# Modulation units inside an RWKV-7 stage: four k-tiles per transfer, their four products as one group

## The chip, the cores and the metric

The kernel runs on one core of a Trainium2 chip. The metric is the device time of one execution in microseconds (us); the median of three executions before the change is 2456.73 us. Below, PE is the matrix engine (TensorE), PEld its weight loads, DVE VectorE, ACT ScalarE, POOL GpSimd, and SP the engine whose queue issues most transfers (DMAs) from DRAM.

## The reference

One layer of a hybrid model on 256 latent tokens and 256 context tokens of width 2048. A vector `c` scales, shifts and gates the layer's branches (modulation):

```
mod_lat = jnp.split((silu_c @ w_mod[i] + b_mod[i])[:, None, :], 6, axis=-1)
u_lat = _modulate(_rmsnorm(x, g_norm1[i]), mod_lat[0], mod_lat[1])
...
x = x + mod_lat[2] * y_lat
v_lat = _modulate(_rmsnorm(x, g_norm2[i]), mod_lat[3], mod_lat[4])
x = x + mod_lat[5] * _moe(v_lat, *moe_p)
```

`w_mod` is a float32 matrix of 2048 x 12288, 96 MB. Its first third (`mod_lat[0]`, `mod_lat[1]`) is needed before anything else. The other two thirds, 64 MB, are needed only after the token mixer, and that part is what the change touches. The token mixer has three branches: S5 (a state-space scan), RWKV-7 (a recurrence with a 64 x 64 state for each of 16 heads, in two directions) and gated linear attention; a mixture of experts follows.

## The kernel before

The program is written as Python generators that yield after each small piece of work. `merge` runs several of them side by side: it always steps the one that has done the smallest share of the steps it is taken to have. The order so written is only a preference. A scheduler behind it puts the instructions of each engine into a fixed order, taking what it believes to be ready first, in the order of writing among those. Each engine then works through its own list strictly in order and waits at semaphores.

**The RWKV-7 stage** (`rwkv`) merges five streams, over 18 steps and one before them:

- `dense`: products of the normed tokens with columns of `w_in`. `split` loads a block of four k-tiles of weights (`ww`, 256 KB, line 346, on SP), ACT casts it to a shortened float `hw` (line 348), DVE forms the remainder `lw` (line 353), and PE multiplies three times for each k-tile (lines 384 to 386). The pools hold four raw blocks, three `hw` and three `lw`, so loads and splits run some blocks ahead of PE, and a load waits until an earlier block has been split.
- `rw_build1` and `rw_build2`: the operators of a half (one channel tile, latents or context), small products on PE with much work on DVE, ACT and POOL between them.
- `rw_chain`: the recurrence of the half before, a chain that goes through PE, DVE and POOL for every chunk of 32 tokens.
- `mods`: the rest of the modulation.

**`mods`** handles 16 units, each 512 columns of `w_mod`. The vector silu(c) is the stationary operand, as one column in a window of 32 columns (`self.sil[:, k, win]`); the weights stream past it. The array is used in four column groups of 32: k-tile k goes to the group `k % 4`, written `tile_position=(0, 32 * j)`, and its result is added in the quadrant `pt[32 * j:32 * j + 32]` of one PSUM bank. Unit u lands in row u of each quadrant, because the window is shifted by u. For each unit, eight blocks of two k-tiles (`wm`, 512 KB each, line 952) come in on SP. Two places rotate for them (`wm=2` in `BUFS`). In every other block of the first 15 units, the two k-tiles are scaled and added first, on ACT (line 956) and DVE (line 957), and one product with a column of ones (`self.one`, line 960) follows:

```
nc.scalar.activation(w[:, 1], w[:, 1], AF.Copy, scale=c[1])
nc.vector.scalar_tensor_tensor(w[:, 1], w[:, 0], c[0], w[:, 1], op0=OP.mult, op1=OP.add)
```

The other blocks have two products, one for each k-tile (line 969). Each product is float32 and shows as two records in the trace. So there are 60 blocks with one product and 68 with two: 196 products in 128 places of PE's list. `rwkv` gives `mods` 18 of its steps in each step of the stage (`chainv(mods, 18)`), and a unit has 17.

The first third of the modulation is done by `mod_unit` at the start of the program, with the same products (line 254) and no sums.

Of the kernel before, what the change touches and what calls it, by code (L numbers as in the profile page):

```python
# [11 lines left out]
AF = mybir.ActivationFunctionType  # L12
OP = mybir.AluOpType
# [7 lines left out]
# columns of the packed per-channel parameters  # L21
# [15 lines left out]
def mergeg(*streams):  # L37
    """Runs generators side by side, each given with the number of steps it is taken to have."""
    live = [[g, 0, max(n, 1)] for g, n in streams if g is not None]
    while live:  # L40
        s = min(live, key=lambda x: x[1] / x[2])
        try:
            next(s[0])
            s[1] += 1
            yield
        except StopIteration:
            live.remove(s)
# [7 lines left out]
# places of the blocks of the experts' weights: first pool, later pool, and those that lend their place at the start  # L55
MW, MWB, MWC = 14, 3, 3
# tiles that rotate
BUFS = dict(raw=4, wh=3, wl=3, wm=2, dl=3, z=2, kb=2, vz=2, t1=2, S=2, lmk=2, lmr=2, dup=2, ar0=2)
# [11 lines left out]
def chainv(g, n):  # L70
    """the first n steps of a generator"""
    for _ in range(n if g is not None else 0):
        if next(g, StopIteration) is StopIteration:
            return
        yield


def late(g, n):
    """a generator after n empty steps"""
    if g is None:  # L80
        return
    for _ in range(n):
        yield
    yield from g


class Pool:
    """tiles that share a place by name"""
# [8 lines left out]
# where a tile lives, if not among RWKV-7's  # L97
TOP = ("pp", "ident", "ones", "eps", "id32", "hsel")
MID = ("hka", "hb", "nmu", "omk", "sil", "one")
# [6 lines left out]
class Kern:  # L106
# [29 lines left out]
    # ---------------------------------------------------------------- constants  # L136
    def consts(self):
# [14 lines left out]
        # ident folded on 32 columns: 1 where the column is the partition modulo 32  # L152
# [3 lines left out]
        # rows of the two heads of a channel tile  # L156
# [8 lines left out]
        # the latents' in a column of zeros, for windows that put it into a row of its own  # L165
# [3 lines left out]
        self.one = self.t([128, 47], "one")  # L169
        nc.vector.memset(self.one, 0.0)  # L170
        nc.vector.memset(self.one[:, 15:16], 1.0)
        # derived parameters
# [10 lines left out]
    def rwkv_consts(self):  # L183
        nc = self.nc
        # sum of the free index and the partition: 127 on the other diagonal
# [3 lines left out]
        # position within a chunk: partition modulo 32 (pr) and column modulo 32 (cr)  # L189
# [8 lines left out]
        # parity of the quadrant: 1 even, -1 odd  # L198
# [6 lines left out]
        # source on the partition, target on the column: strictly before (0, 1); not after (2, 3), minus where the  # L205
        # removed keys lie
# [6 lines left out]
        # the diagonal, for each parity  # L213
# [4 lines left out]
        # blocks of 16: the same; below the diagonal, row block odd, column block the one before it  # L218
# [13 lines left out]
        # the diagonal of blocks  # L232
# [4 lines left out]
        # restarts of the running sum, every 32 tokens  # L237
# [4 lines left out]
    # ---------------------------------------------------------------- modulation  # L242
    def mod_unit(self, pt, n):
        """pt[32j + r, :] = silu(c_r) . w_mod[:, 512 n ...] over the k-tiles of group j"""
# [13 lines left out]
    def mod_out(self, pt, n):  # L258
        """the unit's columns on partitions, into modT"""
# [10 lines left out]
    def phase_a(self, jobs):  # L270
# [12 lines left out]
        def norm():  # L283
            # root mean squares of the tokens, on every partition
# [19 lines left out]
        # the first columns of w_in as far as the normed tokens are there  # L304
# [36 lines left out]
    # ---------------------------------------------------------------- dense products  # L341
    def split(self, src, shape, name):
        """A block of weights from DRAM as two float32r parts whose sum it is."""
# [6 lines left out]
        # now and then on Pool, where the vector engine has more to do  # L350
# [5 lines left out]
    def dense(self, jobs, nk=16, xs=None, kb=4):  # L356
        """Columns of products as channels on partitions. Jobs: (source [128, nk, m] by k-tiles, n, evac(psum)) with n
        tokens; the blocks of weights are split ahead of their products."""
# [32 lines left out]
    # ---------------------------------------------------------------- RWKV-7  # L391
    def mix(self, z, ns, col, tag):
        """z + (prev - z) mu for both directions, the second with its time reversed.
        z [128, ns, 258] has a zero before and after each sequence; the result [128, ns, 2, 256]."""
# [15 lines left out]
    def rw_lo(self):  # L410
        """the low-rank inputs of decay and learning rate"""
        def ev(pt):
# [5 lines left out]
            # in two parts one below the other, per head of the two  # L418
# [11 lines left out]
    def wcol(self, name, i, n, evac, m=128):  # L430
        """a job of dense: columns of w_in, [2, 128, 8, m]"""
# [3 lines left out]
    def rw_cols(self, ct):  # L435
        """key, value and receptance of a channel tile"""
# [7 lines left out]
    def rank_up(self, ct):  # L444
        """the second factors of decay and learning rate for a channel tile, in two parts"""
# [9 lines left out]
    def rw_build1(self, ct, s):  # L455
        """chunk operators of the two heads of a channel tile: s = 0 the latents, 1 the context.
        Chunk c of a row of four (j): what belongs to the keys lies in quadrant c, what belongs to the removed keys
        in quadrant c ^ 1, so that both are neighbours in the half that holds c, in the tile e = c % 2."""
# [10 lines left out]
        # gates of this channel tile  # L469
# [9 lines left out]
        # sigmoid(x) = (1 + tanh(x / 2)) / 2; the second is kept as its tanh  # L479
# [6 lines left out]
        # the key that is removed, and the inverse square of its norm  # L486
# [14 lines left out]
        # running log decay of each chunk, and its exponentials  # L501
# [13 lines left out]
        # alpha, and rho beside it for the latents, the chunks in the order 1 0 3 2 ...  # L515
# [8 lines left out]
        # the key scaled by the learning rate  # L524
# [3 lines left out]
        # beta: the removed key over its squared norm, times the learning rate  # L528
# [21 lines left out]
        # products of the keys with alpha (0, 1) and rho (2 + e), sources on partitions, masked by time  # L550
# [22 lines left out]
        if lat:  # L573
            # the bonus of the current token joins the diagonal
# [7 lines left out]
        # kappa and minus beta in the frame of the chunk's end: [e][j][half][slot][t]  # L582
# [12 lines left out]
    def rw_build2(self, ct, s):  # L595
        """the rest of them: rows by token, the inverse of the removed keys' products and what goes through it"""
# [25 lines left out]
        # the four chunks of a row side by side, zero elsewhere  # L622
# [9 lines left out]
        # removed values of the chunk's own: (alpha kappa) v, alpha beside it  # L632
# [7 lines left out]
        # inverse of 1 + L, transposed: blocks of 16 by substitution, then doubled  # L640
# [31 lines left out]
        # the half blocks below the diagonal; narrow operands on the left, so that four products share the array: each  # L672
        # product swaps the rows' quadrants with the columns' rows of chunks
# [24 lines left out]
        # through the inverse  # L698
# [12 lines left out]
        # the state's part of the removed values per chunk  # L711
# [4 lines left out]
    def rw_chain(self, ct, s):  # L716
        """the states from chunk to chunk, both directions; after the latents' the outputs"""
# [11 lines left out]
        for c8 in range(8):  # L729
# [4 lines left out]
            else:  # L734
# [9 lines left out]
                # S D  # L744
# [15 lines left out]
            elif c8 == 7:  # L760
                # the states at the chunks of the latents
# [1389 lines left out]
```

## Time and profile before

| What | us |
| --- | --- |
| Median of three executions | 2456.73 |
| Lowest and highest of them | 2451.40, 2471.96 |
| Span of the profiled execution, first to last instruction | 2446.7 |
| PE busy in it | 2233.6 |
| DVE busy in it | 1492.1 |
| ACT busy in it | 957.4 |
| First and last transfer of `mods` issued | 680.6, 1564.2 |

The profiled execution's own time is given only as its span; the median lies 10.0 us above it, which holds what happens ahead of the first and behind the last instruction, and the spread between executions. Times inside the trace count from the first instruction. PE busy is the union of the records of products; ends of products are modelled, so two products that follow each other overlap a little in the records, and the distance from start to start is the better measure of what one costs.

### The profile page before, as it was taken

The page shows a single profiled execution, that of the slowest core. Times are in us where ns is not written, and L with a number is a line of the kernel's source. Part 1 is how long each engine was busy: PE and PEld are TensorE (multiplying, and loading weights), DVE is VectorE, ACT ScalarE, POOL GpSimd, SP SyncE. Part 2 cuts the span into 40 slices and gives each one's busy share as a digit, 9 for nine tenths or more (in the row PEclk, how much of TensorE's full clock was granted, in tenths as well). Part 3 has the DMA queues.
Part 4 walks back from the last instruction along what each step waited for, and adds up shares of the span by engine and source line. Part 5 has one row for each costly group of instructions (what it writes and reads, how often), then busy time and mean ns, then how long its engine had stood idle before and what let it go on. Part 6 is the DMA issues. An engine that isn't in the chain of part 4 may idle for free. (4 is left out here: it accounts for less than half of the span.)

```text
span 2446.7 us, 49814 instructions
## 1 busy us (share of the span) xinstructions
PE 2233.6 (91%) x19197; PEld 1567.3 (64%) x19197; DVE 1492.1 (61%) x3878; ACT 957.4 (39%) x1893; POOL 450.7 (18%) x705
## 2 busy tenths in 40 slices
PE   7899989988999999999999999999998988887774
PEld 2447667766677777777777777788997753332210
DVE  8955967867667777777777767686765432211112
ACT  2235234246555444454444454453553431111111
POOL 2422033120213222322222222221011000000000
PEclk9999999989999999999999999999999989998888
DMA  7763432443374545454545454454667799999997
GB/s 288 286 217 100 125 111 86 126 142 97 92 247 162 178 139 182 141 180 142 181 141 186 140 179 141 154 167 153 210 204 253 247 371 422 421 421 422 420 422 303
DMA packets 189750, 526.06 MB, mean 215 GB/s; under 512 B 22401, under 2 KB 48017, under 8 KB 164545
## 3 DMA queue, kind: packets, MB, share of 16 engines
q1 hardware_dynamic: 173488, 500.15, 57.7%
q10 hardware_dynamic: 14160, 16.36, 1.9%
q0 software_dynamic: 1856, 6.29, 0.7%
q8 instruction: 153, 2.51, 0.4%
q14 instruction: 93, 0.75, 0.1%
HBM read 502.16 MB, written 19.51 MB: 213 GB/s over the span
## 5 line engine op out<-in xcount | busy, mean ns | idle before, releaser
L348 ACT CAST hw<-ww 128x512 fp32r<-128x512 f32 x556 | 340.1, 616 | 619.8 <-PE pd L385 517.6
L384 PE MATMUL pd<-UH,hw 128*128 128x256 f32 (+2 forms) x1648 | 563.1, 342 | 12.4 <-DVE fo L900 9.1
L386 PE MATMUL pd<-UH,lw 128*128 128x256 f32 (+2 forms) x1648 | 536.8, 326 | 12.0 <-DVE lw L353 8.9
L385 PE MATMUL pd<-UL,hw 128*128 128x256 f32 (+2 forms) x1648 | 533.1, 324 | 0.0
L353 DVE TENSOR_TENSOR lw<-ww,hw 128x512 fp32r<-128x512 f32 x544 | 384.9, 710 | 192.1 <-ACT hw L348 184.8
L384 PEld LDWEIGHTS pd<-UH,hw 128*128 128x128 f32 (+1 forms) x1648 | 312.1, 189 | 136.4 <-issue 71.9
L386 PEld LDWEIGHTS pd<-UH,lw 128*128 128x128 f32 (+1 forms) x1648 | 311.8, 189 | 55.6 <-DVE lw L353 16.0
L385 PEld LDWEIGHTS pd<-UL,hw 128*128 128x128 f32 (+1 forms) x1648 | 312.4, 190 | 30.0 <-issue 7.2
L1887 ACT ACTIVATE xg<-pm,modT,a 128x128 f32<-128x128 f32 x128 | 46.2, 484 | 306.8 <-PE pe L1911 283.8
L1911 PE MATMUL pe<-mw,xg 128*32 128x512 f32 x1024 | 135.4, 645 | 27.5 <-DMA mw<-in_moe_gu_dram 27.3
L1911 PEld LDWEIGHTS pe<-mw,xg 128*32 128x32 f32 x1024 | 27.7, 112 | 108.9 <-DMA mw<-in_moe_gu_dram 62.6
L1991 POOL TENSOR_TENSOR acc<-acc,mw 128x512 f32<-128x512 f32 x2 | 3.4, 1717 | 480.1 <-ACT acc L1990 480.1
L1932 PE MATMUL pdn<-mw,ht 128*32 128x512 f32 x512 | 81.3, 691 | 5.8 <-ACT ht L1925 3.3
L1940 PE MATMUL pm<-ysl,owt 128*128 128x512 f32 x128 | 63.5, 618 | 20.4 <-DVE ysl L1937 20.4
L741 DVE TENSOR_TENSOR vz<-psa,z 32x256 f32<-32x256 f32 x120 | 50.2, 418 | 47.6 <-PE psa L738 45.7
L1884 PEld LDWEIGHTS pm<-oh,m 128*128 128x128 f32 x512 | 61.1, 196 | 25.5 <-issue 25.5
L1920 DVE TENSOR_TENSOR hd<-hd,pe 128x256 f32<-128x256 f32 x8 | 3.4, 422 | 119.5 <-ACT hd L1919 119.5
L254 PE MATMUL pmod<-wm,silu 128*32 128x512 f32 x256 | 62.3, 646 | 14.8 <-DMA wm<-in_w_mod_dram 14.2
L969 PE MATMUL pmod<-wm,sil 128*32 128x512 f32 x272 | 75.3, 604 | 0.0
L353 DVE TENSOR_TENSOR lx<-wx,hx 128x512 fp32r<-128x512 f32 x64 | 43.6, 691 | 51.5 <-ACT hx L348 50.3
L386 PE MATMUL pd<-XAh,lw 128*128 128x256 f32 x256 | 72.4, 283 | 2.6 <-DVE lw L353 2.6
L384 PE MATMUL pd<-XAh,hw 128*128 128x256 f32 x256 | 73.8, 288 | 0.2 <-ACT sg L1266 0.2
(584 smaller groups left out, 4506.0 us busy)
## 6 DMA issues: line engine op xcount, KB each, us to landing
mw<-in_moe_gu_dram SPq DMA_DIRECT2D x128, 1024.0 KB, 19.7
wm<-in_w_mod_dram SPq DMA_DIRECT2D x192, 512.0 KB, 4.2
mw<-in_moe_d_dram SPq DMA_DIRECT2D x64, 1024.0 KB, 19.7
ww<-in_w_gate_dram SPq DMA_DIRECT2D x192, 256.0 KB, 3.1
ww<-in_w_cols_dram SPq DMA_DIRECT2D x132, 256.0 KB, 3.0
ww<-in_w_rkv_dram SPq DMA_DIRECT2D x96, 256.0 KB, 3.2
ww<-in_glu_dram SPq DMA_DIRECT2D x64, 256.0 KB, 3.0
wx<-in_w_out_dram SPq DMA_DIRECT2D x64, 256.0 KB, 4.9
```

Of the source, the lines that this page charges most:

```text
L254: nc.tensor.matmul(pt[32 * j:32 * j + 32, :], self.silu[:, k, :], w[:, k2, :], start=k < 4, stop=k >= 12, tile_position=(0, 32 * j))
L348: nc.scalar.copy(h, w)
L353: eng.tensor_tensor(l, w, h.bitcast(FT), op=OP.subtract)
L384: nc.tensor.matmul(ov, h[:, k2, :], uh, start=k == 0, stop=False)
L385: nc.tensor.matmul(ov, h[:, k2, :], ul, start=False, stop=False)
L386: nc.tensor.matmul(ov, l[:, k2, :], uh, start=False, stop=k == nk - 1)
L741: nc.vector.tensor_tensor(vz[bq, e, tt::2, :].rearrange(V, h=2), psa[bq, :, 0:128].rearrange("p h (d v) -> p h d v", d=2), z[bq, tt::2, :] ...
L969: nc.tensor.matmul(pt[32 * j:32 * j + 32, :], self.sil[:, k, win], w[:, k2], start=j not in begun, stop=u == 15 and k >= 12, tile_position ...
L1884: nc.tensor.matmul(p[:, 128 * (k % 4):128 * (k % 4) + 128], self.x2[:, t, 128 * k:128 * k + 128], oh[:, t, :], start=t == 0, stop=t == 1)
L1911: nc.tensor.matmul(pe[32 * e:32 * e + 32, :], xg[:, k, 32 * e:32 * e + 32], w[:, e, :], start=k == 0, stop=k == 15, tile_position=(0, 32 * e))
L1932: nc.tensor.matmul(py[32 * e:32 * e + 32, :], ht[:, f, 32 * e:32 * e + 32], w[:, e, :], start=f == 0, stop=f == 1, tile_position=(0, 32 * e))
L1940: nc.tensor.matmul(pr, owt[:, 128 * t:128 * t + 128], ys, start=True, stop=True)
```

## The change

`mods` now goes through a unit in four groups of four k-tiles. One transfer of 1 MB brings the four (`wm`, two blocks of the DRAM layout side by side); one place is left for it, as large as the two were together. Six empty steps follow, then the four products, one for each column group, written inside `high_priority()`, which lets the scheduler take them ahead of anything else that is ready; then six more empty steps. The sums on ACT and DVE and the column of ones are gone, so all 256 products are made, in 64 places. `chainv(mods, 45)` gives 45 steps in each step of the stage; a unit now has 48. Comments are dropped as well, so line numbers of the changed kernel differ.

```diff
-BUFS = dict(raw=4, wh=3, wl=3, wm=2, dl=3, z=2, kb=2, vz=2, t1=2, S=2, lmk=2, lmr=2, dup=2, ar0=2)
+BUFS = dict(raw=4, wh=3, wl=3, dl=3, z=2, kb=2, vz=2, t1=2, S=2, lmk=2, lmr=2, dup=2, ar0=2)
...
+def idle(n):
+    for _ in range(n):
+        yield
...
-        self.one = self.t([128, 47], "one")
-        nc.vector.memset(self.one, 0.0)
-        nc.vector.memset(self.one[:, 15:16], 1.0)
...
-                  (half(self.rw_chain, i - 1), 18), (chainv(mods, 18), 18))
+                  (half(self.rw_chain, i - 1), 18), (chainv(mods, 45), 45))
...
-        begun = set()
         for u in range(16):
             win = slice(15 - u, 47 - u)
-            for kq in range(8):
-                w = self.t([128, 2, 512], "wm")
-                nc.sync.dma_start(w, self.A["w_mod"][8 + u, kq])
-                if u < 15 and kq % 2 == 0:
...
-                    nc.scalar.activation(w[:, 1], w[:, 1], AF.Copy, scale=c[1])
-                    nc.vector.scalar_tensor_tensor(w[:, 1], w[:, 0], c[0], w[:, 1], op0=OP.mult, op1=OP.add)
...
-                    nc.tensor.matmul(pt[32 * j:32 * j + 32, :], self.one[:, win], w[:, 1], start=j not in begun,
-                                     stop=False, tile_position=(0, 32 * j))
...
-                for k2 in range(2):
-                    k = 2 * kq + k2
-                    j = k % 4
-                    nc.tensor.matmul(pt[32 * j:32 * j + 32, :], self.sil[:, k, win], w[:, k2], start=j not in begun,
-                                     stop=u == 15 and k >= 12, tile_position=(0, 32 * j))
...
+            for kq in range(0, 8, 2):
+                w = self.t([128, 4, 512], "wm")
+                nc.sync.dma_start(w.rearrange("p (q a) b -> p q a b", q=2),
+                                  self.A["w_mod"][8 + u, kq:kq + 2].rearrange("q p a b -> p q a b"))
+                yield from idle(6)
+                with self.tc.high_priority():
+                    for j in range(4):
+                        nc.tensor.matmul(pt[32 * j:32 * j + 32], self.sil[:, 2 * kq + j, win], w[:, j],
+                                         start=u == 0 and kq == 0, stop=u == 15 and kq == 6,
+                                         tile_position=(0, 32 * j))
+                yield from idle(6)
```

The order of the instructions moves as well. On PE, in the middle of the stage of the kernel before, a block's two products (`L969`, x2) stand between products of `dense` (`pd`), operators and the recurrence:

```order
L386 MATMUL pd<-UH,lw 128x256
L62 MATMUL pm<-ident,kbs 128x128 x4
L384 MATMUL pd<-UH,hw 128x256
L385 MATMUL pd<-UL,hw 128x256
L386 MATMUL pd<-UH,lw 128x256
L754 MATMUL pu<-vz,kb 64x64 x4
L969 MATMUL pmod<-wm,sil 32x512 x2
L384 MATMUL pd<-UH,hw 128x256
```

On PE of the changed kernel, early in the stage, `L958` is the product of `mods`, and `L386` to `L388` are the products of `dense`:

```order
L388 MATMUL pd<-UH,lw 128x512
L62 MATMUL pm<-ident,nb 128x128 x4
L688 MATMUL pm<-xd,lmk 32x128 x8
L386 MATMUL pd<-UH,hw 128x512
L387 MATMUL pd<-UL,hw 128x512
L388 MATMUL pd<-UH,lw 128x512
L958 MATMUL pmod<-wm,sil 32x512 x4
L548 MATMUL pm<-hsel,pr 128x2 x4
L386 MATMUL pd<-UH,hw 128x512
```

Four products now stand together where there were one or two; apart from them, the rows of PE keep their sequence closely.

On SP of the kernel before, loads of `wm` (`L952`, 512 KB) alternate with loads of `dense` (`L346`, 256 KB) through nearly the whole stage. These are ten rows of it:

```order
L346 DMA ww<-in_w_gate_dram 128x512 x2
L952 DMA wm<-in_w_mod_dram 128x1024
L346 DMA ww<-in_w_gate_dram 128x512 x3
L952 DMA wm<-in_w_mod_dram 128x1024
L346 DMA ww<-in_w_gate_dram 128x512
L952 DMA wm<-in_w_mod_dram 128x1024
L346 DMA ww<-in_w_gate_dram 128x512 x2
L952 DMA wm<-in_w_mod_dram 128x1024
L346 DMA ww<-in_w_rkv_dram 128x512 x5
L952 DMA wm<-in_w_mod_dram 128x1024
```

On SP of the changed kernel (`L953`: `wm`, 1 MB; `L348`: `ww`; `L450`: a small load of `rw_build1`), these rows hold the last three loads of `mods` and what follows:

```order
L348 DMA ww<-in_w_rkv_dram 128x512
L953 DMA wm<-in_w_mod_dram 128x2x1024
L348 DMA ww<-in_w_rkv_dram 128x512 x2
L953 DMA wm<-in_w_mod_dram 128x2x1024
L348 DMA ww<-in_w_gate_dram 128x512 x2
L450 DMA waup<-in_waup_dram 128x512
L348 DMA ww<-in_w_gate_dram 128x512 x10
L348 DMA ww<-in_w_rkv_dram 128x512 x4
```

About two loads of `dense` still stand between two loads of `mods`, but each of those is now twice as large. Between the first and the last load of `mods`, 262 loads of `dense` stand on SP before the change and 137 after it: the modulation now lies in the first half of the stage, and the second half has none.

## Rows read from the trace of the kernel before

**Rows 1.** The page: busy us, share of the span and instructions of each engine.
```profile
PE 2233.6 (91%) x19197; PEld 1567.3 (64%) x19197; DVE 1492.1 (61%) x3878; ACT 957.4 (39%) x1893; POOL 450.7 (18%) x705
```

**Rows 2.** Busy time by stretch: while mods runs, and the 120 us behind.
```profile
core 0: us, PE busy (x) PEld busy (x) DVE busy (x) ACT busy (x) POOL busy (x), PEclk, DMA share, GB/s
680.00:1580.00 900.00, 891.97 (x9422) 677.74 (x9421) 645.71 (x1824) 441.39 (x854) 232.38 (x464) 1.00 0.52 167
1580.00:1700.00 120.00, 116.48 (x1505) 104.91 (x1504) 92.28 (x250) 55.79 (x106) 28.10 (x58) 1.00 0.47 147
```

**Rows 3.** Groups by line and form, 680 to 1580: busy us, mean ns, idle before.
```profile
L348 ACT CAST hw<-ww 128x512 fp32r<-128x512 f32 x268 | 165.2, 618 | 328.1 <-PE pd L385 314.7 <-DVE lw L353 4.4 <-DMA ww<-in_w_gate_dram 3.2
...
L969 PE MATMUL pmod<-wm,sil 128*32 128x512 f32 x272 | 75.3, 604 | 0.0
L960 PE MATMUL pmod<-wm,one 128*32 128x512 f32 x120 | 62.7, 604 | 4.0 <-DVE wm L957 3.7
...
L957 DVE SCALAR_TENSOR_TENSOR wm<-wm,sil 128x512 f32<-128x512 f32 x60 | 47.8, 797 | 8.3 <-ACT wm L956 7.6
...
L956 ACT ACTIVATE wm<-wm,sil 128x512 f32<-128x512 f32 x60 | 43.2, 720 | 20.7 <-DMA wm<-in_w_mod_dram 20.6
```

**Rows 4.** Timeline of PE around one place of mods: start us, us, line.
```profile
1001.63 0.40 PE L385 MATMUL pd<-UL,hw 128*128 128x512 f32 x1
1001.95 1.05 PE L960 MATMUL pmod<-wm,one 128*32 128x512 f32 x2
1002.93 0.50 PE L386 MATMUL pd<-UH,lw 128*128 128x512 f32 x1
1003.27 0.40 PE L384 MATMUL pd<-UH,hw 128*128 128x512 f32 x1
1003.50 0.39 PE L385 MATMUL pd<-UL,hw 128*128 128x512 f32 x1
```

**Rows 5.** Timeline of PE in mod_unit, where four products came together (x8).
```profile
152.13 0.40 PE L317 MATMUL pd<-UH,lw 128*128 128x512 f32 x1
152.46 1.07 PE L254 MATMUL pmod<-wm,silu 128*32 128x512 f32 x8
153.45 0.50 PE L315 MATMUL pd<-UH,hw 128*128 128x512 f32 x1
153.79 0.39 PE L316 MATMUL pd<-UL,hw 128*128 128x512 f32 x1
```

**Rows 6.** Loads of mods on SP (L952): issue and landing.
```profile
L952 SPq DMA_DIRECT2D wm<-in_w_mod_dram x128: 327/328/1278, 680.6 to 1564.2; - x128
...
DMA to landing us min/median/max: 3.3/3.9/6.5
```

**Rows 7.** Tile xop: two loads of 1 MB, at 1612.7 and 1621.0 us.
```profile
L1169 SPq DMA_DIRECT2D xop<-dxc x1: 327/327/327, 1612.7 to 1612.7; - x1
...
DMA to landing us min/median/max: 5.0/5.1/5.1
```

**Rows 8.** The page: GB/s in 40 slices, and issues with KB and us to landing.
```profile
GB/s 288 286 217 100 125 111 86 126 142 97 92 247 162 178 139 182 141 180 142 181 141 186 140 179 141 154 167 153 210 204 253 247 371 422 421 421 422 420 422 303
...
mw<-in_moe_gu_dram SPq DMA_DIRECT2D x128, 1024.0 KB, 19.7
```

**Rows 9.** Waits of SP's queue, 680 to 1580: us, times, longest us.
```profile
SPq L346 <- DVE lw L353: 257.1, 122, 5.0
SPq L952 <- PE pmod L969: 153.1, 62, 7.5
SPq L952 <- PE pmod L960: 122.3, 51, 8.0
```

More of the change, by code (lines that the diff above doesn't have):

```diff
@@ L98 @@
 TOP = ("pp", "ident", "ones", "eps", "id32", "hsel")
-MID = ("hka", "hb", "nmu", "omk", "sil", "one")
+MID = ("hka", "hb", "nmu", "omk", "sil")
 WTS = ("raw", "wh", "wl")
@@ L946, in mods @@
         pt = self.ps.tile([128, 512], FT, tag="mod", name="pmod")
-        begun = set()
         for u in range(16):
             win = slice(15 - u, 47 - u)
-            for kq in range(8):
-                w = self.t([128, 2, 512], "wm")
-                nc.sync.dma_start(w, self.A["w_mod"][8 + u, kq])
-                if u < 15 and kq % 2 == 0:
-                    c = [self.sil[:, 2 * kq + k2, 15:16] for k2 in range(2)]
-                    nc.scalar.activation(w[:, 1], w[:, 1], AF.Copy, scale=c[1])
-                    nc.vector.scalar_tensor_tensor(w[:, 1], w[:, 0], c[0], w[:, 1], op0=OP.mult, op1=OP.add)
-                    yield
-                    j = kq % 4
-                    nc.tensor.matmul(pt[32 * j:32 * j + 32, :], self.one[:, win], w[:, 1], start=j not in begun,
-                                     stop=False, tile_position=(0, 32 * j))
-                    begun.add(j)
-                    yield
-                    continue
-                yield
-                for k2 in range(2):
-                    k = 2 * kq + k2
-                    j = k % 4
-                    nc.tensor.matmul(pt[32 * j:32 * j + 32, :], self.sil[:, k, win], w[:, k2], start=j not in begun,
-                                     stop=u == 15 and k >= 12, tile_position=(0, 32 * j))
-                    begun.add(j)
-                yield
-            yield
+            for kq in range(0, 8, 2):
[9 more added lines that the diff above has]
+                yield from idle(6)
         e = self.t([128, 512], "w1", name="e_mod")
```

## The prediction

> **What bounds the kernel now.** I read the page first: PE is busy 91% of the span, no other engine above 64% [rows 1]. An average says nothing about one stage, so I cut out the stretch in which `mods` runs, 680 to 1580 us: PE is busy 891.97 of 900 us, DVE 645.71, ACT 441.39, and the transfers take 0.52 of what the DMA engines offer [rows 2]. The granted clock there is 1.00, that is the higher of its two levels, 2.4 GHz. So in this stage time is what PE's list takes, and the groups by line tell what of it belongs to the modulation [rows 3]: 75.3 us for the products of line 969 and 62.7 us for those of line 960, 138.0 together. The same group rows show who waits: ACT's cast for `dense` sat idle 314.7 us until PE had used up a block, and only 3.2 us until weights had landed. Loads and splits run ahead of PE and wait for it. The waits of SP say the same for `mods` [rows 9]: 62 + 51 = 113 of its 128 loads stood on SP until PE had finished a product of `mods`.
>
> **What a place in PE's list costs.** In the timeline, one product of line 960 stands between products of `dense` [rows 4]. From the last `dense` start before it (1001.63) to the second one after it (1003.27) are 1.64 us. Without it these would be two steps of `dense`, each 0.23 us (1003.27 to 1003.50). The place costs 1.64 - 0.46 = 1.18 us: 0.98 for the product (1001.95 to 1002.93) and 0.20 for going into and out of the narrow form. How dear is a place with four products? `mod_unit` shows it where four happened to come together, eight records [rows 5]: 153.79 - 152.13 = 1.66 us, less 0.46, is 1.20 us; and from the first start to the next `dense` start are 0.99 us. Four column groups run beside each other and cost what one costs.
>
> The Trainium skill has a rule against that, in "TensorE: Matmul & The Clock Gate", section "Measured speedup vs the span model": three column tiles were measured at 2.38 times, not 3, which would be an estimate of 3 / 2.38 x 0.98 = 1.24 us for a group. The rows on four products do not bear it out (0.99 us); by that rule the sum below would lose about 64 x 0.25 = 16 us.
>
> **The change part by part.**
>
> 1. *Fewer places on PE.* Before: 60 places with one product, 68 with two, 128 x 1.18 = 151 us. After: 64 x 1.20 = 77 us. That frees 74 us. A lower bound comes from the busy times: 138.0 - 64 x 1.07 = 70 us; a few places stood side by side and shared the 0.20. I take -72. All of it is on the path as long as PE is the bound.
>
> 2. *The sums go.* 60 instructions on DVE (47.8 us) and 60 on ACT (43.2 us) [rows 3]. Both engines are idle over a quarter of the stage, and PE's work hides them: nothing, except the one wait that PE had on them, 4.0 us before line 960. I take -4. If PE were not the cover, up to 47.8 us of DVE's time would count.
>
> 3. *One place for 1 MB in place of two for 512 KB.* This is the added wait. The next load can start only when the four products are through, and the four products after that can start only when it has landed, with everything in PE's list behind them: `dense`, the operators, the recurrence. So what counts is PE's other work between two groups, against load time. In the order, 262 loads of `dense` lie between the first and last load of `mods` before, and 137 after. Before, the stretch took 1564.2 - 680.6 = 884 us [rows 6], less 151 for `mods` is 733 us, or 2.80 us for a block. After, 137 / 64 = 2.14 blocks lie between two groups: 6.0 us of other work. I also priced the rows between each two groups of the new order by the mean distance of starts that such a row has in the trace: 4.9 to 7.6 us, mean 6.2. How long does 1 MB take? No load of `mods` shows it. Two loads of 1 MB in a calm stretch took 5.0 and 5.1 us [rows 7]; 512 KB took 3.3 us at best [rows 6], so 512 KB more cost 1.7 us, and a `ww` of 256 KB just ahead some 0.9. I take 5.1 + 0.8 = 5.9 us, a little under the work that covers it. Then the shortest intervals, those under 5.9, lack some 7 us in all, and scatter in landing makes it more: I take +12. Ends: nothing, if 5.1 holds; and if the queue were as full as in the experts' stage (19.7 us for 1 MB at 420 GB/s [rows 8]), 64 x 13.7 = 877 us. The stage runs at 167 GB/s [rows 2]. In the first half it would be 64 loads of 1 MB and 137 of 256 KB, 103 million bytes in some 470 us, 219 GB/s, plus some writes. That is far nearer to the low end.
>
> 4. *SP.* The load of `mods` waits on SP, and the `ww` behind it wait with it. That is not new: SP stood 275 us at these loads before [rows 9], and it cost ACT 3.2 us of waiting for weights [rows 3]. The new order puts as many blocks (mostly six) between the products that free the place and the load as the old one. A `ww` behind 1 MB in place of 512 KB lands up to 1.7 us later, against casts that wait for PE. I take 0; at most ACT's wait would double, 3 us.
>
> 5. *The second half has no groups.* There PE's list holds only `dense` and the recurrence, denser, and less lies between a result on DVE and the product that needs it. The stretch just behind the last load shows how that looks: 3.5 us idle in 120 [rows 2], against 8.0 in 900. Over the remaining 350 us or so that would be 10 - 3 = 7 us. I take +6, between 0 and 10.
>
> Sum: -72 - 4 + 12 + 0 + 6 = -58 us. The profiled execution has a span of 2446.7 us and would become 2388.7. The median of the runs lies 10.0 above the span, so I forecast 2456.7 - 58 = 2398.7, rounded 2399 us. Nothing behind the stage moves against it: the experts' stage, bound by its transfers, begins earlier by as much.
>
> **The rivals.**
>
> *A. The load becomes the bound (slower).* Place: PE's wait for `wm` ahead of the first of four products. For it speaks that 512 KB has taken up to 6.5 us in this stage [rows 6], when others were in flight; with 1.7 us for the second half, 8.2 us for 1 MB. If that were typical, each cycle would lack 8.2 - 6.0 = 2.2 us, 64 x 2.2 = 141 us in place of the 12: -72 - 4 + 141 + 6 = +71, 2528 us. It turns from gain to loss at 6.0 + 70 / 64 = 7.1 us for a load. Against it: the median of 512 KB is 3.9, and a waiting PE also stops asking for `ww`, which empties the queue. The Trainium skill, "Trainium Kernel Development and Optimization", section "Best Practices", advises two buffers so that transfers overlap work, and the change gives one up. By that rule this rival would be the outcome; the trace agrees only if PE's other work between the groups is shorter than a load.
>
> *B. The chain through DVE takes over.* If the recurrence sets the pace once PE has less to do, the second half keeps its pace, and about half the gain goes: -29, 2428 us. For it: DVE is busy 72% of the stage, and 77% in the 120 us behind [rows 2]. Against it: even there PE is busy 97%.
>
> *C. Four products do not run beside each other here.* If two pairs ran one after the other, a group would cost 0.98 more, 63 us in all: -58 + 63 = +5, 2462 us. The eight records in 0.99 us speak against it [rows 5].
>
> **How the numbers follow.** Chances: forecast 0.70, A 0.08, B 0.16, C 0.03, and 0.03 for a gain beyond 80 us, if the relief of DVE and ACT is worth more than nothing. The forecast's own range is -78 (load hidden, second half free) to -33 (load 6.4 us): 2378 to 2424 us. The range for 8 in 10 goes down to 2374 and up to 2440, into B. A measurement of this kernel can tell about 1% from no change: faster means below 2432, slower above 2481. Forecast, gain beyond and two thirds of B give 0.83 faster; C, the rest of B and 0.01 of A 0.10 the same; the rest of A 0.07 slower.
>
> **What would show it.** Right: eight records of line 958 in some 1.05 us busy, 64 times, 67 to 70 us in all; the last of them at about 1150 us; PE busy over 98% of the stage, which ends 58 us earlier; PE's wait for `wm` about 12 us; loads of 1 MB landing in 5 to 6 us at the median. Wrong on term 3: a median landing over 7 us and waits of PE for `wm` of 1 us and more at each group. Wrong on term 5: PE busy under 95% from 1150 us on, with waits for DVE. Wrong on term 1: records of line 958 that start 0.5 us or more apart within a group.

## The result, and the profile after

The changed kernel takes 2427.33 us at the median of eight executions (2421.58 to 2445.61), the kernel before 2455.48 in eight on the same chip (2445.78 to 2471.96). The ratio is 0.99 [0.9878, 0.9921]: the change saves some 25 us (28 between the medians), where 58 were forecast. The profiled execution took 2429.91 us, 1.9 above its span; the 10.0 that the forecast carried from span to median was mostly spread between executions.

From the page of the changed kernel, its span and the busy times:

```profile
span 2428.0 us, 49729 instructions
...
PE 2202.4 (91%) x19317; PEld 1582.0 (65%) x19317; DVE 1451.3 (60%) x3816; ACT 922.8 (38%) x1833; POOL 440.3 (18%) x705
```

Against [rows 1] PE lost 31.2 us of busy time, DVE 40.8, ACT 34.6. The span fell by 18.7 only, so PE must now be idle where it was not. The windows tell in which half of the stage, columns as in [rows 2]:

```profile
680.00:1160.00 480.00, 457.92 (x4909) 345.55 (x4908) 301.54 (x867) 205.85 (x401) 106.50 (x230) 0.99 0.68 229
1160.00:1560.00 400.00, 394.73 (x4714) 340.87 (x4713) 310.41 (x920) 204.27 (x400) 114.87 (x236) 1.00 0.33 102
```

While the groups run, PE is idle for 22.1 of 480 us; before, 8.0 in the whole 900 [rows 2]. What it waits for stands in the group row of the products (680 to 1580, columns as in [rows 3]):

```profile
L958 PE MATMUL pmod<-wm,sil 128*32 128x512 f32 x512 | 68.2, 605 | 21.6 <-DMA wm<-in_w_mod_dram 21.3
```

and in PE's waits, with total, times and longest:

```profile
PE pmod L958 <- DMA wm<-in_w_mod_dram: 21.3, 21, 2.5
PE psa L740 <- DVE S L770: 2.6, 4, 0.6
```

A third of the 64 groups wait for their own transfer. In [rows 3] the products of line 969 had no idle time in front of them at all.

For a clock inside the stage I take `dyb`, a transfer that POOL issues when the recurrence of a channel tile is done: eight points that every version passes. Here is how far apart three of them lie, two tiles, in the kernel before (first and last start behind the colon):

```profile
L800 POOL DMA_DIRECT2D dyb<-yo x3: 719/723/744, 1023.0 to 1270.5; - x3
```

and in the changed kernel, first where groups run, then behind them:

```profile
L802 POOL DMA_DIRECT2D dyb<-yo x3: 726/742/755, 915.3 to 1178.0; - x3
L802 POOL DMA_DIRECT2D dyb<-yo x3: 722/723/726, 1178.0 to 1394.4; - x3
```

A tile took 123.8 us before. It takes 131.4 with groups in it and 108.2 without. The first half of the stage has become slower than it was (the third of the eight points lies at 1178.0 us, before at 1146.6), and all of the gain is made in the second. The last of the eight points moved from 1701.3 to 1675.3, by 26.0 us. The profiled execution lost 7.3 of it again behind the stage; the medians, 28.2 apart, show no such loss.

### The profile page after: what moved, and what is told of

Its sections match the earlier page's. It is cut to its first block, busy times and chain, and to the rows that moved or that the text cites. A ratio compares the mean times of both kernels' runs of the same rounds, so it can differ in the third digit from the quotient of the medians.

```text
span 2428.0 us, 49729 instructions
## 1 busy us (share of the span) xinstructions
PE 2202.4 (91%) x19317; PEld 1582.0 (65%) x19317; DVE 1451.3 (60%) x3816; ACT 922.8 (38%) x1833; POOL 440.3 (18%) x705
## 5 line engine op out<-in xcount | busy, mean ns | idle before, releaser
L386 PE MATMUL pd<-UH,hw 128*128 128x256 f32 (+2 forms) x1648 | 566.0, 343 | 8.8 <-ACT hw L350 4.4
L388 PE MATMUL pd<-UH,lw 128*128 128x256 f32 (+2 forms) x1648 | 543.3, 330 | 10.1 <-DVE lw L355 7.0
L387 PE MATMUL pd<-UL,hw 128*128 128x256 f32 (+2 forms) x1648 | 538.8, 327 | 0.0
L386 PEld LDWEIGHTS pd<-UH,hw 128*128 128x128 f32 (+1 forms) x1648 | 314.3, 191 | 62.0 <-issue 14.1
L388 PEld LDWEIGHTS pd<-UH,lw 128*128 128x128 f32 (+1 forms) x1648 | 314.7, 191 | 57.7 <-DVE lw L355 13.6
L958 PE MATMUL pmod<-wm,sil 128*32 128x512 f32 x512 | 68.2, 605 | 21.6 <-DMA wm<-in_w_mod_dram 21.3
L388 PE MATMUL pd<-XAh,lw 128*128 128x256 f32 x256 | 73.3, 286 | 3.5 <-DVE lw L355 3.5
L386 PE MATMUL pd<-XAh,hw 128*128 128x256 f32 x256 | 74.0, 289 | 0.0
```

The lines of the kernel that those rows point to most:

```text
L386: nc.tensor.matmul(ov, h[:, k2, :], uh, start=k == 0, stop=False)
L387: nc.tensor.matmul(ov, h[:, k2, :], ul, start=False, stop=False)
L388: nc.tensor.matmul(ov, l[:, k2, :], uh, start=False, stop=k == nk - 1)
L958: nc.tensor.matmul(pt[32 * j:32 * j + 32], self.sil[:, 2 * kq + j, win], w[:, j], start=u == 0 and kq == 0, stop=u == 15 and kq == 6, tile ...
```

## The experiments

**1. Groups spread over the stage.** Theory: the 1 MB transfers come too close together for one place, and the wait is what is missing. Each group is held until the product of `dense` written just ahead of it, so that the scheduler cannot draw groups together:

```diff
-                nc.tensor.matmul(ov, l[:, k2, :], uh, start=False, stop=k == nk - 1)
+                self.lastmm = nc.tensor.matmul(ov, l[:, k2, :], uh, start=False, stop=k == nk - 1)
...
-                with self.tc.high_priority():
+                with self.tc.issue_after(getattr(self.lastmm, "ins", self.lastmm)), self.tc.high_priority():
```

> The changed kernel, with each group of four products queued on PE behind the product of dense written last before it, so that groups spread over the whole stage, with at least 9 us of PE's other work between two of them from the third on, in place of some 6. Nothing else is changed and nothing is left out. Theory (PE waits for the 1 MB load, since 6 us of other work do not cover its landing and the release of its one place): the wait of PE and PEld for wm, 21 and 28 us in the changed kernel, falls under 6 us, and the time falls by 20 to 30 us against the changed kernel, to 2397 to 2407 us. Rival (what was lost in the first half comes from the denser transfers or from the price of the places and not from the order): waits of another kind take their place, and the time stays within 8 us of the changed kernel's 2427.

Measured: 2411.83 us, ratio 0.9843 [0.9817, 0.9868]. In its trace PE's wait has gone:

```profile
PE pmod L958 <- DMA wm<-in_w_mod_dram: 1.3, 1, 1.3
```

The wait was real and on the path. But by the ratios the run is 14 us faster than the changed kernel; the theory had 20 to 30, the rival under 8. And without the wait the gain is 38 us, not the 70 that the forecast without its term 3 would give. So there is more than the wait; run 4 and runs 9 to 11 look for it.

**2. Groups in the order of writing.** The other way to draw groups apart: `high_priority()` taken away, so that products go where the text has them.

```diff
-                with self.tc.high_priority():
-                    for j in range(4):
-                        nc.tensor.matmul(pt[32 * j:32 * j + 32], self.sil[:, 2 * kq + j, win], w[:, j],
...
+                for j in range(4):
+                    nc.tensor.matmul(pt[32 * j:32 * j + 32], self.sil[:, 2 * kq + j, win], w[:, j],
```

> The changed kernel without the raised priority of the four products. The groups spread over the stage as in the run before, but eight of them are cut in two by other products, so 72 places on PE in place of 64. Theory (a place costs about 1 us): 8 us slower than the run with whole groups, 2405 to 2415 us. Rival (the raised priority itself makes the gain): no faster than the changed kernel, 2427 us or more.

Measured: 2418.02 us, 0.9865 [0.9834, 0.9896]: 3 us above the theory's range, 9 below the rival's. PE waits 4.2 us for `wm`, three times. In the trace nine groups are cut in two by other products, 73 places in all. That run 2 is slower than run 1 for it is not shown: it is 5 us by the ratios, and the intervals overlap.

**3. The kernel before without its sums.** All pairs get two products; the branch with ACT, DVE and the column of ones is gone. That gives 12 more places (140), since some pairs of products are parted by others in the new order.

```diff
-                if u < 15 and kq % 2 == 0:
...
-                    c = [self.sil[:, 2 * kq + k2, 15:16] for k2 in range(2)]
-                    nc.scalar.activation(w[:, 1], w[:, 1], AF.Copy, scale=c[1])
-                    nc.vector.scalar_tensor_tensor(w[:, 1], w[:, 0], c[0], w[:, 1], op0=OP.mult, op1=OP.add)
...
```

> The kernel before with only the sums of pairs of k-tiles dropped: all 256 products, two of them in each place, loads of 512 KB in two places of the pool as before. Places on PE stay about 128 (the order cuts some pairs: 140). Theory (ACT and DVE were not the bound, a place costs the same with one product or two): between 6 us faster (PE's 4 us of waits for the sums) and 10 us slower (12 more places), 2449 to 2465 us. Rival (the 91 us of DVE and ACT were worth something): over 12 us faster, under 2443 us.

Measured: 2460.16 us, 1.0039 [1.0022, 1.0056], 9.6 us slower than before. Twelve places at the 0.91 us of the next run are 10.9. So 91 us of work on DVE and ACT [rows 3] were worth some 1 us of time: PE's list hid them, as term 2 had it.

**4. Eight groups of 64.** What is a place worth? Only units 0 and 15 are computed; the rest of this part of the modulation is left out.

```diff
-        for u in range(16):
+        for u in (0, 15):
```

> The changed kernel with only units 0 and 15 of the 16 that mods handles: 8 groups in place of 64; the rest of the modulation behind the first third is left out. It prices a place. Theory (a place costs 1.18 us as in the timeline, and 22 of the waits for the load go): 56 x 1.18 + 22 = 88 us faster than the changed kernel, 2339 us. Rival (going into and out of the narrow form is not given back, so a place is worth 0.95 us or less): 56 x 0.95 + 22 = 75 us faster, 2352 us or more.

Measured: 2349.89 us, 0.9588 [0.9559, 0.9616], so 101 us below the kernel before, not some 116. The median alone does not price a place, for the eight groups that are left still wait 6.7 us for `wm`, which both the theory and the rival had let go. The tiles behind them do. Two tiles without groups take as long here as in the second half of the changed kernel:

```profile
L802 POOL DMA_DIRECT2D dyb<-yo x3: 719/726/742, 994.6 to 1211.3; - x3
```

216.7 us, against 247.5 before with 34 places in them: 30.8 / 34 = 0.91 us for a place, where the forecast took 1.18. The theory fell.

**5 to 7. How far apart?** As run 1, with more steps of `mods` for each step of the stage, so that the groups come closer (the edit of run 6, with 60; runs 5 and 7 have 50 and 90):

```diff
-                  (half(self.rw_chain, i - 1), 18), (chainv(mods, 45), 45))
+                  (half(self.rw_chain, i - 1), 18), (chainv(mods, 60), 60))
```

> The spread groups of the first run with 50 steps of the modulation in each step of the stage in place of 45: PE's other work between two groups is 12.8 us in the mean (14.2 before), and the last group stands behind the 417th load of dense in place of the 450th, so none lies behind the recurrence's last steps. Theory (the first run gave back some 6 us of places and 8 us of waits behind the stage because its last six groups lay there): wait for wm under 8 us, and 4 to 12 us faster than the first run, at 0.979 to 0.983 of the kernel before. Rival (what is given back behind the stage comes from the branches that follow, whatever the groups do): within 3 us of the first run, 0.983 to 0.986.

> The same with 60 steps: 10.6 us of other work between two groups in the mean, but 6 to 7 us at some. Theory (PE waits where the work between two groups is shorter than a load and its release): wait for wm on PE 3 to 8 us, time as in the run with 50 steps within 6 us. Rival (the raised priority and not the distance makes PE wait): no wait, under 2 us.

> The same with 90 steps: 7.0 us of other work between two groups in the mean, most between 5.1 and 7.3, nearly the distance of the changed kernel (6.2). Theory (the distance decides): the wait for wm on PE comes back to 10 to 20 us, and the time to within 8 us of the changed kernel, 0.986 to 0.991 of the kernel before. Rival (the order of the changed kernel is worse than its distance): no more than 5 us of wait and 0.984 or less.

| Steps of `mods` for each of the stage | Last group at, us | PE's wait for `wm`, us (times) | Median, us | Ratio |
| --- | --- | --- | --- | --- |
| 45 (run 1) | 1628.2 | 1.3 (1) | 2411.83 | 0.9843 [0.9817, 0.9868] |
| 50 | 1543.7 | 6.5 (3) | 2409.20 | 0.9818 [0.9797, 0.9839] |
| 60 | 1409.2 | 8.7 (6) | 2403.28 | 0.9798 [0.9777, 0.982] |
| 90 | 1199.4 | 18.5 (20) | 2426.97 | 0.9907 [0.9885, 0.9929] |
| changed kernel | 1158.7 | 21.3 (21) | 2427.33 | 0.99 [0.9878, 0.9921] |

Run 5 lies in its theory's range, but its interval reaches the rival's. In run 6 the wait came, a little above the 3 to 8 us of its theory, so that rival fell. With 90 steps the groups lie nearly where the changed kernel has them, and the wait and the time are nearly its own. So it is the distance, not the wait on another product, that decides. Why 60 steps with some waiting are no worse than 45 with hardly any, the two profiled executions don't show; the one with 60 steps was the slowest of its four (2409.79 us). One thing that speaks for it is counted below.

**8. Half the bytes.** Each transfer brings two k-tiles (512 KB), and each is used twice; half of the weights are left out.

```diff
-                w = self.t([128, 4, 512], "wm")
+                w = self.t([128, 2, 512], "wm")
...
-                        nc.tensor.matmul(pt[32 * j:32 * j + 32], self.sil[:, 2 * kq + j, win], w[:, j],
+                        nc.tensor.matmul(pt[32 * j:32 * j + 32], self.sil[:, 2 * kq + j, win], w[:, j % 2],
```

> The changed kernel with loads of 512 KB in place of 1 MB: each group loads two of its four k-tiles only and streams each of them twice; the other half of the weights is left out. The scheduler then sets the groups closer, 4.3 us of other work between two in the mean in place of 6.2. Theory (the order leaves as much time as the scheduler takes a load to need, so scatter in landing makes PE wait whatever its size): the wait for wm stays, 10 us or more, and the time within 10 us of the changed kernel. Rival (1 MB is too much for one transfer, 512 KB lands in 3.9 us and is covered): the wait falls under 5 us and the time by 15 us or more.

Measured: 2421.07 us, 0.9882 [0.9857, 0.9906]. PE still waits 13.7 us, 18 times, though the transfers land in 4.0 us:

```profile
PE pmod L957 <- DMA wm<-in_w_mod_dram: 13.7, 18, 1.7
```

The scheduler set the groups closer again, for it expected the smaller load sooner: the last group starts at 1039.3 us, not 1158.7. A faster transfer does not buy slack when the order is drawn from the time it is taken to need. The run says little on the price of the bytes themselves.

**9 to 11. Where a place is cheap.** In the timeline of before, most places stand beside a small product of the recurrence, not between two of `dense` as the one I had priced [rows 4]. Here is such a place:

```profile
1097.18 0.28 PE L386 MATMUL pd<-UH,lw 128*128 128x256 f32 x1
1097.39 0.42 PE L738 MATMUL psa<-sh,wl 64*32 64x64 f32 x8
1097.74 1.04 PE L960 MATMUL pmod<-wm,one 128*32 128x512 f32 x2
1098.71 0.38 PE L384 MATMUL pd<-UH,hw 128*128 128x256 f32 x1
1098.93 0.28 PE L385 MATMUL pd<-UL,hw 128*128 128x256 f32 x1
```

and the same place in the second half of the changed kernel, where `mods` is through:

```profile
1203.99 0.28 PE L388 MATMUL pd<-UH,lw 128*128 128x256 f32 x1
1204.20 0.42 PE L740 MATMUL psa<-S,wl 64*32 64x64 f32 x8
1204.55 0.38 PE L386 MATMUL pd<-UH,hw 128*128 128x256 f32 x1
1204.78 0.28 PE L387 MATMUL pd<-UL,hw 128*128 128x256 f32 x1
```

The steps of `dense` beside the small product are 0.21 and 0.22 or 0.23 in both, in place of 0.12. From its start to the second `dense` start behind it are 1.54 us with the place and 0.58 without: the place costs 0.96. The 0.20 for a change of form is there anyway. Run 9 takes the kernel before and sets its places behind products of `dense`, where `lastmm` is the last of them that was written (and line 960's product likewise):

```diff
-                for k2 in range(2):
-                    k = 2 * kq + k2
...
+                with self.tc.issue_after(getattr(self.lastmm, "ins", self.lastmm)), self.tc.high_priority():
+                    for k2 in range(2):
+                        k = 2 * kq + k2
...
```

Runs 10 and 11 set the spread groups behind small products of the recurrence, at every fourth or third of them (the edit of run 10):

```diff
+                        self.lastmm = nc.tensor.matmul(psa[bq, h, 64 * d:64 * d + 64], wl[hss[h], 2 * d + tt, c ^ 1, :], S[hss[h], d, :],
...
+                self.nsm += 1
...
+                    self.lastmm = nc.tensor.matmul(pu[hss[h], 64 * d:64 * d + 64], kb[half, e, 2 * d + tt, hss[h]],
...
+            self.nsm += 1
...
+                  (half(self.rw_chain, i - 1), 18), (chainv(mods, 80), 80))
...
+                for _ in range(14):
+                    if self.nsm >= self.usm + 4:
+                        break
+                    yield
+                self.usm = self.nsm
+                m = self.lastmm if self.lastmm is not None else self.lastd
+                with self.tc.issue_after(getattr(m, "ins", m)), self.tc.high_priority():
```

> The kernel before, its 128 places of the modulation kept with their sums, but each product held until the dense product written just ahead of it and put right behind it: in PE's order 119 places stand behind a product of dense, where 39 did. Theory: a place between two dense products costs its own 0.98 us and 0.20 for going into and out of the narrow form; behind another small product the 0.20 is paid anyway. 80 places more that pay it, 80 x 0.20 = 16 us: ratio 1.004 to 1.009, some 2462 to 2474 us against 2452. Rival: what stands ahead of a place does not matter, and the 0.91 us that a place was worth comes from elsewhere: no difference, ratio 0.998 to 1.002.

> The spread groups of four again (through the same stretch as in the first spread version, 0.9843), but each held until a small product of the recurrence and put right behind it: 58 of the 64 groups stand behind one, where all 64 stood behind a product of dense. Theory: 58 x 0.20 = 12 us less than the first spread version, ratio 0.977 to 0.982, some 2396 to 2408 us against 2452, with waits of PE for wm under 5 us. Rival: what stands ahead of a group does not matter: 0.983 to 0.987, 2410 us and more.

> As the run before it, but a group at every third small product in place of every fourth: 52 of 64 groups behind a small product, the last at about the place where the best spread version (0.9798) had its last; six times two groups stand only 25 rows apart. Theory: 50 x 0.20 = 10 us less than the best spread version, and some 5 us more of waiting for wm: ratio 0.975 to 0.980, 2391 to 2403 us. Rival: what stands ahead does not matter, and the closer groups wait: 0.981 to 0.985.

Run 9: 2453.25 us, 0.9999 [0.998, 1.0018]. Run 10: 2396.5 us, 0.9789 [0.9761, 0.9817]. Run 11 (as run 10, with 3 in place of 4): 2397.01 us, 0.977 [0.9746, 0.9793]. Run 9 went to the rival, 10 and 11 to the theory. What separates them is that the theory had counted the wrong thing. In run 9 the places stand behind `dense`, but mostly straight ahead of a small product:

```profile
1036.17 0.28 PE L386 MATMUL pd<-UH,lw 128*128 128x256 f32 x1
1036.38 1.05 PE L961 MATMUL pmod<-wm,one 128*32 128x512 f32 x2
1037.36 0.46 PE L754 MATMUL pu<-vz,kb 64*64 64x64 f32 x8
1037.74 0.38 PE L384 MATMUL pd<-UH,hw 128*128 128x256 f32 x1
```

So no change was added there; the neighbour only went to the other side: 37 places have `dense` on both sides in run 9, and 35 had before. What counts is how often PE goes from anything else into `dense`. Over the same 6000 rows of PE's order that is 421 times before, 429 in run 9, 427 in the changed kernel, 451 in run 1, 431 with 60 steps, 408 and 405 in runs 10 and 11, and 400 in run 4. Eight changes more in run 9 are 1.6 us at 0.20, too little to be seen; 43 fewer in run 10 than in run 1 are 8.6 us, and 0.9843 - 0.9789 of 2452 us is 13. In run 10 PE also waits nowhere for `wm` in the stage, so the count need not be all of it:

```profile
L967 PE MATMUL pmod<-wm,sil 128*32 128x512 f32 x512 | 68.2, 605 | 0.0
```

The counts were made after the results; no run was made to test them alone. But the tiles of the runs bear them out. Here are two tiles of run 1 and two of run 10, without a wait for `wm` and with as much `dense` as the two of run 4:

```profile
L802 POOL DMA_DIRECT2D dyb<-yo x3: 719/723/726, 1116.8 to 1349.8; - x3
L805 POOL DMA_DIRECT2D dyb<-yo x3: 719/723/723, 1108.7 to 1339.0; - x3
```

Run 4 took 216.7 us with no group and 96 changes into `dense`, run 10 takes 230.3 with 16 groups and 98, run 1 takes 233.0 with 15 groups and 110. So a group is 0.85 us in run 10 and 1.09 in run 1; at 0.85 a group, the 12 changes more in run 1 are 3.5 us, some 0.3 each. What makes them dear, the form of the product, its number format or its weight load, these runs don't tell apart.

Runs 10 and 11 beat both kernels. They are not told apart from each other, and run 11 is told from the best of the earlier ones (0.9798) only barely, if at all.

## Why the prediction was wrong, and where it was right

**Term 1, fewer places, was mis-sized.** It took 1.18 us for each of 128 places, from one piece of the timeline, and the piece was not typical. Of the 1.18, the 0.98 of the product itself holds. The 0.20 holds too, but it is paid for a change between `dense` and anything else, and most places before shared one with a small product. The forecast let 64 such changes go, 12.8 us; in the order they went from 421 to 427. So 64 fewer places are 64 x 0.98 = 63 us, and 6 x 0.20 = 1 less: -62, not the -72 taken. It also shows in the busy time of two tiles. Before and after (without groups):

```profile
1023.00:1270.50 247.50, 246.92 (x2654) 187.33 (x2653) 176.70 (x505) 120.38 (x233) 65.58 (x132) 1.00 0.51 162
```

```profile
1178.00:1394.40 216.40, 213.65 (x2553) 183.77 (x2552) 167.67 (x491) 109.75 (x217) 63.51 (x132) 1.00 0.33 102
```

33.3 us of PE's work for 34 places. Of it 1.6 are changes into `dense` (104 in the first window, 96 in the second), which leaves 0.93 for a place itself, a little under the 0.98; by that the term is -58. PE's idle time rises by 2.2 us, from 0.6, and the 33.3 less these 2.2 give the 0.91 of run 4.

**Term 3, one place for 1 MB, was mis-sized too: 21 us of waiting, 25 with the clock of this execution, not 12.** Its means were right: the transfers land in 5.4 us at the median, where the forecast took 5.9:

```profile
DMA to landing us min/median/max: 4.8/5.4/8.4
```

Other work between two groups was 6.1 us on the mean (7.47 from group to group, less 1.06 for the group and 0.3 of wait). But a wait is what a late transfer lacks against a short interval, and nothing is paid back where it is early. The scatter makes it, and that I had put at 5 us without working it out. The sign that was set for this term, a median landing over 7 us, looked at the mean case as well and did not show. The longest wait is an example of a late one. On SP (start, duration, line), the transfer of this group is issued at 1046.64, 1.3 us behind a `ww`:

```profile
1045.31 0.34 SPq L348 DMA_DIRECT2D ww<-in_w_gate_dram  x1
1046.64 0.38 SPq L953 DMA_DIRECT2D wm<-in_w_mod_dram  x1
1050.20 2.07 SPq L348 DMA_DIRECT2D ww<-in_w_gate_dram  x2
```

On PE (start, duration, line, in brackets the idle time before) the group stands at 1054.41, 7.8 us later, and all of `dense` behind it:

```profile
1051.60 0.28 PE L388 MATMUL pd<-UH,lw 128*128 128x256 f32 x1
1054.41 1.06 PE L958 MATMUL pmod<-wm,sil 128*32 128x512 f32 x8 [2.53 <-DMA wm<-in_w_mod_dram]
1055.41 0.39 PE L386 MATMUL pd<-UH,hw 128*128 128x256 f32 x1
```

This execution paid a second price, that no term had. Behind two of the long waits the granted clock falls for a few microseconds, from 2.4 to 1.2 GHz. These are the windows behind the wait above:

```profile
1056.00:1058.00 2.00, 2.00 (x16) 1.67 (x14) 0.69 (x1) 1.01 (x2) 0.00 (x0) 0.50 0.66 135
1058.00:1060.00 2.00, 2.00 (x15) 1.88 (x13) 0.29 (x1) 0.19 (x1) 0.40 (x1) 0.69 1.02 417
```

Over 680 to 1160 us the windows of 10 us lack 0.9, 2.5 and 1.7 us of clock, at 720 to 740 and at 1050 to 1060, each time behind a wait of over 2 us; before, 1.7 us in the whole stage. So 21.3 + 5.1 - 1.7 = 25 us. That each such wait costs clock is not shown. With 90 steps (run 7) PE waits 18.5 us, 2.8 at the longest, and the clock stays up:

```profile
680.00:1200.00 520.00, 500.72 (x5389) 382.51 (x5389) 336.53 (x969) 228.95 (x449) 123.69 (x256) 1.00 0.65 221
```

The fall of the kernel before, at 819 us, stands behind an idle time of 1.6 us that has nothing to do with `wm`. The Trainium skill, "Trainium Kernel Development and Optimization", section "Best Practices", advises two buffers so that transfers overlap work. The trace agrees in part: with one, PE waits 21.3 us, but spread groups live with one at 1.3 us of waiting (run 1). Two places of 1 MB were not tried, so what the second would give in this order is open.

**Term 2, the sums**, -4: run 3 puts it at some -1, give or take 4, so the -4 is not excluded; PE's list hid the rest. **Term 4, SP**, 0: right. ACT's casts still wait for PE, and a late `ww` is not among the first three that end their idle time:

```profile
L350 ACT CAST hw<-ww 128x512 fp32r<-128x512 f32 x281 | 173.4, 619 | 324.1 <-PE pd L387 301.2 <-issue 7.3 <-DVE Y L660 3.7
```

**Term 5, the second half**, +6: right in kind and near in size. By the windows above, two tiles without groups have 2.2 us more of idle time, some 4 us for the four tiles that have none.

With the measured sizes the sum is -62 - 1 + 25 + 4 = -34, against -26.0 at the last of the eight points and some -25 by the ratio. With 0.93 for a place it is -30. The 4 to 8 us that are left are not a dearer group. The two tiles with groups above took 46.3 us more than two without, with 33.5 groups, 6.3 us of waiting for `wm` and 1.7 us of clock in them, which is 4.8 us more than 1.0 for a group. But PE goes into `dense` 112 times there, not 96, which is 3.2 us at 0.20, and has six to eight more products of `dense` of 512 columns there, some 1.6 us at 0.23, which are missing later. That is the 4.8. The sum has these changes in its count of 427, and the products only lie earlier, so where its last 4 to 8 us lie stays open.

**What held.** Eight records in 1.06 us, 68.2 us in all (67 to 70 forecast); the last group at 1158.7 us (1150); transfers that land in 5 to 6 us. PE busy over 98% did not come: 457.92 of 480 us with groups are 95%. Rival C fell with the first: four products cost what one costs, 1.00 us to the next start in place of 0.98. The Trainium skill, "TensorE: Matmul & The Clock Gate", section "Measured speedup vs the span model", has a measured factor of 2.38 for three column tiles, and a span model by which each further tile adds about 4 ns. The trace is near the model, 0.02 us for three further tiles, and the factor is no price for a group in this list. Rival B fell: the second half went at 108.2 us a tile and was not held back. That its 2428 us is nearly the time measured is chance. Rival A was the right mechanism at a fifth of its price, 25 us and not 141: the load did not become the bound, but it became a wait.

## What to carry to other kernels

A transfer with a single buffer is to be priced by its late cases against the short intervals, not mean against mean; and when a scheduler draws the work together to the time it believes a load takes, holding each group a little further apart can be worth nearly as much as the change itself (0.99 became 0.980 to 0.984 here, and 0.977 to 0.979 with small products as neighbours too). A price read off one piece of a timeline is to be tried on several neighbourhoods: ask which part of it the neighbours pay anyway.

## What the runs showed of the hardware

- A 1 MB transfer of `wm` lands in 4.8 to 8.4 us in the changed kernel, 4.7 to 7.4 in run 1, where groups lie far apart: even spread out, it varies by over a half of its shortest time.
- Between a small product and `dense` about 0.10 us is lost (a step of 256 columns takes 0.12 us in `dense`). Behind every kind of small product the first step takes 0.20 to 0.23, in two tiles. Ahead of the narrow ones (`psa`, `pu`, `pg`) the last step takes 0.21, ahead of `pm` mostly 0.12. It is paid once for a whole run of them: small products that stand together share it.
- In the changed kernel's stretch with groups the granted clock fell to 0.50 for some 7 and 3 us behind idle times of PE of 2.17 and 2.53 us, which lost 5.1 us; a wait of 1.65 us at 789 us left it at 1.00. In the kernel before it fell behind one of 1.6 us, and in run 7 one of 2.8 us left it at 1.00. So the length of the idle time alone did not decide.
